# When the blocks of a seven-product pair are loaded: the fifth made unit's block one unit in front of the pair, and one group of sums one unit later

## The chip, the cores and the metric

The kernel runs on one core of a Trainium2 chip. The metric is the device time of one execution in microseconds. The kernel before has a median of 2097.52 us over three runs (2096.82 to 2102.56); its profiled execution took 2096.35 us, of which 2094.6 us are the profile's span.

## The reference

Two transformer layers over 256 tokens of 2048 channels, in float32. What matters here is the multilayer perceptron at the end of each layer, which reads two matrices of 2048x8192 and 8192x2048:

```python
def sq_relu_mlp(h, g, w1, w2):
    a = jax.nn.relu(rms_norm(h, g) @ w1)
    return (a * a) @ w2

h = h + o.reshape(B, S, D) @ a_w_out[l]
h = h + sq_relu_mlp(h, mlp_norm_g[layer], mlp_w1[layer], mlp_w2[layer])
```

In front of each perceptron stands an attention with its projections (a causal one with a forget gate in the first layer, a chunked one with a relative bias in the second), and between the layers one K/V projection. The change touches the two perceptrons alone.

## The kernel before

**Units.** All weights stream from memory. A weight tile of 128x1024 is a unit. ScalarE rounds it to `hi` (line 218), VectorE subtracts to get `lo` (line 219), and TensorE makes three passes, `hi` by the rounded activations (462), `hi` by their rest (464), `lo` by the rounded activations (466). Three `hi` and three `lo` buffers exist, so the splitting can run some units ahead of TensorE and no further. Plain units come into four `raw` buffers by SyncE's queue (line 201), `EARLY` = 3 of them in front of the splitting, which itself is kept `AHEAD` = 2 units in front of the products by `top_up`.

**Pairs.** In the perceptrons the weights are taken two column blocks at a time, a pair, and a pair's first rows are multiplied by a scheme with seven products in place of eight. For it four blocks of the pair, `"11"`, `"12"`, `"21"`, `"22"`, are loaded whole into rooms of their own by `bring` (line 801), and seven made units are formed from them, in the order

```python
self.pair, self.name, self.half = pair, ("11", "T3", "T2", "T1", "21", "T4", "22")[i], half
```

where `T3` = 22 + 12, `T2` = T3 + 11, `T1` = 12 + 11, `T4` = 21 + T2. Pairs are plain (blocks of 128x1024) or wide (128x1536, a second half unit `hih`, `loh` of 512 columns goes with each made unit). In a wide pair VectorE makes `T3` and `T2` (`make`, line 811) while `T1` and `T4` are made by a transfer that adds a block from memory onto a tile (`put`, line 817, GpSimd's queue). In a plain pair VectorE makes all four. All rooms have two buffers to a tag: `"12"` and `"21"` share one tag, `"11"` and `"22"` the other.

**Order around a pair.** `Pair.plan` writes out the order: made units 1 to 4, with the last three plain units of the pair before between them, then the pair's own plain units with made units 5, 6 and 7 among the first of them. The fifth made unit is block `"21"`. Each pair also has a tuple `when`, in the order `("12", "22", "21", "11", "T3", "T1")`, which says how many plain units ahead of the pair's start each block is loaded, or `T3` and `T1` made; `prepare` is called after every plain unit with the count `d` of plain units left and does what is due. Since all engines but GpSimd keep the written order (`keep_order`), a block's load takes a fixed place among the `raw` loads and the small transfers of SyncE's one queue, and it is issued when everything written ahead of it there has been issued; a `raw` load waits there for a buffer that line 219 has to give free.

There are 16 pairs to a perceptron, eight of the first matrix (numbered `i` = 0 to 7, all wide but the first) and eight of the second (the odd ones wide). 15 of the 16 have one of the two tuples that are changed.

**Hidden activations.** When the two accumulators of a column block of the first matrix are complete, `turn_hidden` (the change's second place) turns them through memory (lines 330, 340, 346) and then runs seven steps at given plain units: relu, rounded square, square, rest of the square (line 841), the four sums of activations for the seven-product scheme (lines 285 to 288), their rounding (292), their rest (295). The tuple `uses` holds the units; the first chunk's first two column blocks have tuples of their own, of which one is changed.

Of the kernel before, what the change touches and what calls it, by code (L numbers as in the profile page):

```python
# [33 lines left out]
WIDE1 = (1, 2, 3, 4, 5, 6, 7)  # L34
# [15 lines left out]
def trunk(ctx: ExitStack, tc: tile.TileContext, xT, xr, gs, hg, bf, wgate, w_in, w_oa, w1a, w1fa, w1sa, w2a, w2fa, w2sa,  # L50
# [94 lines left out]
    def plan_mlp(w1, w1f, w1s, w2, w2f, w2s, tail):  # L145
        pairs = []

        def add(w, wf, ws, i, wides, order, when):
            j = wides.index(i) if i in wides else i - sum(1 for k in wides if k < i)
            names = ("11", "12", "21", "22")  # L150
            if i in wides:
                src = [[None] * 3 + [ws[10 * j + 5 * q + u] for u in range(5)] for q in range(2)]
                big = {k: wf[4 * j + m] for m, k in enumerate(names)}
            else:
                src = [[w[16 * j + 8 * q + u] for u in range(8)] for q in range(2)]
                big = {k: src[int(k[1]) - 1][int(k[0]) - 1] for k in names}
            pairs.append(Pair(big, src, order, len(pairs) % 2 == 0, when, i in wides))

        close = (7, 5, 6, 4, 3, 2)
        for c in range(NCH):  # L160
            for q in range(2):
                i = 2 * c + q
                order = "ahead" if i in WIDE1 else "" if i else "early"
                when = (25, 20, 9, 15, 10, 8) if not i else (9, 7, 8, 6, 3, 2) if i == 1 else close if i - 1 in WIDE1 or not q else (9, 7, 8, 6, 5, 1)
                add(w1, w1f, w1s, i, WIDE1, order, when)
            for q in range(2):
                i = 2 * c + q
                add(w2, w2f, w2s, i, WIDE2, "wide" if q else "late", close if q or i + 1 in WIDE1 else (9, 7, 8, 6, 5, 2))
        plan, rest = [], [(tail, 0, u) for u in range(KT // UA - 3, KT // UA)]
        for p in pairs:  # L170
            mine, rest = p.plan(rest)
            plan += mine
        plan += rest
        units.extend(Form(p, i, q == 3) if q > 1 else p.src[q][i] for p, q, i in plan)
        return plan
# [4 lines left out]
    queue(w_oa, n_out)  # L180
    tail_a = Tail(w_oa, n_out - 5)
    plan_a = plan_mlp(w1a, w1fa, w1sa, w2a, w2fa, w2sa, tail_a)
    queue(w_qb, w_qb.shape[0])
    for i in range(w_kv.shape[0]):
        units.append(w_kv[i])
    queue(w_ob, n_out)
    tail_b = Tail(w_ob, n_out - 5)
    plan_b = plan_mlp(w1b, w1fb, w1sb, w2b, w2fb, w2sb, tail_b)
    ready = deque()

# [127 lines left out]
    def steps(make):  # L318
        box = []

        def step():
            if not box:
                box.append(make())
            next(box[0])
        return step

    def blocks32(src, z, b):
        n = src.shape[1] // P
        nb = z.shape[1] // (n * P)
        V.transpose(z.rearrange("p (j n b c) -> p b n j c", j=4, n=n, b=nb)[:, b],  # L330
                    src.rearrange("p (n j c) -> p n j c", n=n, j=4))

    def carry(z, dst, wait=1):
        w = z.shape[1]
        n = w // 4
        box = []

        def rows():
            box.append(dram.tile([P, w], F32, name="turn", tag=f"turn{w}", bufs=4))
            SY.dma_start(box[0], z)  # L340

        def columns():
            s = box[0].rearrange("(i a) f -> a i f", i=4)
            d = dst.rearrange("p (i f) -> p i f", i=4)
            for j in range(4):
                SY.dma_start(d[32 * j : 32 * j + 32], s[:, :, j * n : (j + 1) * n])

        return [[rows]] + [[]] * wait + [[columns], [], []]

    def turned(name=None):  # L350
        z = qkv.tile([P, GH * T], F32, name="z")
        return (z, qkv.tile([P, GH * T], F32, name=name, tag=name, bufs=2)) if name else z
# [310 lines left out]
    def add_fill(items):  # L663
        for i, it in enumerate(items):
            if i < len(fill):
                fill[i] = fill[i] + it
            else:
                fill.append(it)
# [155 lines left out]
    def mlp(plan, x, Sx, st, last):  # L824
# [4 lines left out]
        def take(t, c, n):  # L829
            S.activation(t, t, AF.Relu)  # L830
            y = acts.tile([P, 2, GH, T], F32R, name="act")
            hi, lo = (y[:, i].rearrange("p k (b i c) -> p (k b) i c", b=NB, i=4) for i in range(2))
            t3 = t.rearrange("p (i kb c) -> p kb i c", i=4, c=32)
            yield
            S.activation(hi, t3, AF.Square)
            yield
            S.activation(t, t, AF.Square)
            yield

            def low():  # L840
                V.tensor_tensor(lo, t3, hi.bitcast(F32), op=ALU.subtract)

            hids[c].extend(y[:, :, j, :] for j in range(GH))
            low()
            yield
            if n == 0:
                r = prob.tile([P, 9 * 3 * P], F32R, name="Sh", tag="p", bufs=1)
                Sh[c].extend(r[:, i : i + n] for i, n in ((0, UN), (UN, UN), (2 * UN, 512), (2 * UN + 512, 512)))
                yield from sums([[t3[:, 2 * j + b :: 4] for j in range(2)] for b in range(NB)], Sh[c])
            elif n == 1:  # L850
                yield from sums([[t3[:, 2 * j + b : 2 * j + b + 1] for j in range(2)] for b in range(NB)], Sh[c][2:], 1)

        def turn_hidden(c, n):
            zt = []

            def f(b, ps):
                if b == 0:
                    zt.extend(turned("q"))
                blocks32(ps, zt[0], b)
                if b == NB - 1:  # L860
                    step = steps(lambda: take(zt[1], c, n))
                    uses = ((4, 5, 7, 8, 9, 10, 11), (4, 5, 6, 7, 8, 10, 15), (4, 5, 7, 8), (4, 5, 6, 6))[n]
                    if not c and n < 2:
                        uses = (5, 6, 7, 8, 8, 10, 15) if n else (4, 5, 6, 7, 8, 9, 10)
                    add_fill(carry(*zt, 0)[:2] + [[step] * uses.count(i) for i in range(3, uses[-1] + 1)])
            return f

# [192 lines left out]
```

## Time and profile before

| | |
|---|---|
| median of 3 runs | 2097.52 us (2096.82 to 2102.56) |
| profiled execution | 2096.35 us, span 2094.6 us |
| TensorE matmuls (PE) | 2087.4 us busy, 100% of the span, 9266 of them |
| TensorE weight loads (PEld) | 1726.7 us, 82% |
| VectorE (DVE) | 1606.3 us, 77% |
| ScalarE (ACT) | 1233.0 us, 59% |
| GpSimd (POOL) | 98.2 us, 5% |
| HBM read and written | 250 GB/s over the span |
| granted TensorE clock | 1.00 |

Engine names in the profile are those in brackets; SPq is SyncE's queue of transfers, and L219 is line 219 of the kernel. A row of the timeline has the start and the length in us, the engine, the line, the operation, the tiles it writes and reads, how many equal instructions were merged (x4), and in brackets how long the engine had been idle and what ended that. The length of a matmul there is a modelled one that overlaps its successor; the distance between starts is the pace. A transfer's row shows its issue; it lands later.

### The profile page before, as it was taken

To read this page: it belongs to the slowest core of one execution; us is meant where nothing else is said; L and a number is where in the kernel's file an instruction comes from. 1 tells how busy PE (TensorE), PEld (TensorE's weight loads), DVE (VectorE), ACT (ScalarE), POOL (GpSimd) and SP (SyncE) were. 2 spreads that over 40 slices of the span, in tenths; PEclk is the share of its full clock that TensorE was granted. 3 is DMA by queue.
4 is the path that set the end of the run, shared out by engine and by line. 5 is a ranking of instruction groups with operands and counts; after the bars stand their busy time and mean duration, and the time that the engine had idled before them with its cause. 6 is when DMAs were issued, how large, how long until landed. Compare 5 with 4: busy or idle time off the path is not lost.

```text
span 2094.6 us, 26203 instructions
## 1 busy us (share of the span) xinstructions
PE 2087.4 (100%) x9266; PEld 1726.7 (82%) x9266; DVE 1606.3 (77%) x1920; ACT 1233.0 (59%) x1583; POOL 98.2 (5%) x107
## 2 busy tenths in 40 slices
PE   9999999999999999999999999999999999999999
PEld 7888888888888888888888888887888888888887
DVE  6767666888788778878777677678977887788786
ACT  6544454776566566556675455456755665665664
POOL 1111000000000000000001010000000000000000
PEclk9999999999999999999999999999999999999999
DMA  7787778778787897787778777788787887878875
GB/s 287 246 257 242 228 255 266 250 253 276 250 265 236 260 277 251 220 276 271 230 233 263 236 233 232 240 268 256 250 279 250 243 261 256 269 244 247 275 265 152
DMA packets 181205, 526.25 MB, mean 251 GB/s; under 512 B 36801, under 2 KB 72017, under 8 KB 181073
## 3 DMA queue, kind: packets, MB, share of 16 engines
q1 hardware_dynamic: 173552, 484.69, 68.3%
q0 software_dynamic: 7520, 39.87, 10.2%
q8 instruction: 73, 1.20, 0.2%
q14 instruction: 60, 0.48, 0.1%
HBM read 484.62 MB, written 39.87 MB: 250 GB/s over the span
## 4 chain that ended last, share of the span: by engine, by line
PE 98%; DMA 1%; ACT 0%; DVE 0%; SPq 0%; issue 0%; DVEq 0%; ACTq 0%
PE acc L462 26%; PE acc L464 26%; PE acc L466 26%; PE s L466 6%; PE s L462 6%; PE s L464 6%; PE s L605 1%; PE po L635 1%; DMA raw<-in_w1b 0%; PE s L604 0%; PE po L636 0%; DMA raw<-in_w_in 0%; PE s L727 0%; ACT hi L218 0%; DVE lo L219 0%; DVE act L310 0%
## 5 line engine op out<-in xcount | busy, mean ns | idle before, releaser
L219 DVE TENSOR_TENSOR lo<-raw,hi 128x1024 fp32r<-128x1024 f32 (+1 forms) x598 | 724.7, 1216 | 241.5 <-ACT hi L218 227.0
L218 ACT ACTIVATE hi<-raw 128x1024 fp32r<-128x1024 f32 (+1 forms) x598 | 628.6, 1052 | 318.1 <-PE acc L464 231.7
L462 PE MATMUL acc<-hi,act 128*128 128x512 f32 x2154 | 593.1, 394 | 2.0 <-ACT act L309 1.1
L464 PE MATMUL acc<-hi,act 128*128 128x512 f32 x2154 | 583.8, 389 | 0.1
L466 PE MATMUL acc<-lo,act 128*128 128x512 f32 x2154 | 583.2, 389 | 0.1
L464 PEld LDWEIGHTS acc<-hi,act 128*128 128x128 f32 x2154 | 403.9, 188 | 85.7 <-DVE act L310 0.7
L466 PEld LDWEIGHTS acc<-lo,act 128*128 128x128 f32 x2154 | 403.8, 188 | 85.2 <-DVE lo L219 1.4
L462 PEld LDWEIGHTS acc<-hi,act 128*128 128x128 f32 x2154 | 401.7, 188 | 85.6 <-ACT hi L218 1.7
L218 ACT ACTIVATE hi<-w 128x1024 fp32r<-128x1024 f32 x138 | 145.6, 1055 | 126.3 <-DMA w<-in_w1fb 26.8
L219 DVE TENSOR_TENSOR lo<-w,hi 128x1024 fp32r<-128x1024 f32 x138 | 167.6, 1214 | 54.5 <-ACT hi L218 48.6
L219 DVE TENSOR_TENSOR lo<-wT,hi 128x1024 fp32r<-128x1024 f32 x86 | 104.9, 1219 | 37.0 <-ACT hi L218 36.6
L462 PE MATMUL s<-hi,act 128*128 128x512 f32 x424 | 114.7, 389 | 0.0
L466 PE MATMUL s<-lo,act 128*128 128x512 f32 x424 | 114.6, 389 | 0.0
L464 PE MATMUL s<-hi,act 128*128 128x512 f32 x424 | 114.6, 389 | 0.0
L218 ACT ACTIVATE hi<-wT 128x1024 fp32r<-128x1024 f32 x86 | 90.8, 1056 | 24.8 <-PE acc L464 13.0
L464 PEld LDWEIGHTS s<-hi,act 128*128 128x128 f32 x424 | 79.6, 188 | 16.5
L466 PEld LDWEIGHTS s<-lo,act 128*128 128x128 f32 x424 | 79.4, 188 | 16.7 <-DVE lo L219 0.2
L462 PEld LDWEIGHTS s<-hi,act 128*128 128x128 f32 x424 | 79.5, 188 | 16.5
L218 ACT ACTIVATE hih<-w 128x512 fp32r<-128x512 f32 x88 | 55.2, 627 | 61.0 <-PE acc L464 50.0
L219 DVE TENSOR_TENSOR loh<-w,hih 128x512 fp32r<-128x512 f32 x88 | 60.4, 687 | 19.8 <-ACT hih L218 19.8
L218 ACT ACTIVATE hih<-wT 128x512 fp32r<-128x512 f32 x66 | 41.4, 628 | 57.2 <-PE acc L464 47.9
L638 ACT ACTIVATE act<-po 128x256 fp32r<-128x256 f32 x32 | 12.3, 385 | 86.2 <-PE po L636 86.2
(207 smaller groups left out, 1835.4 us busy)
## 6 DMA issues: line engine op xcount, KB each, us to landing
raw<-in_w_in SPq DMA_DIRECT2D x96, 512.0 KB, 4.5
raw<-in_w1sa SPq DMA_DIRECT2D x70, 512.0 KB, 5.5
raw<-in_w1sb SPq DMA_DIRECT2D x70, 512.0 KB, 5.8
raw<-in_w_kv SPq DMA_DIRECT2D x64, 512.0 KB, 4.6
turn<-z SPq DMA_DIRECT2D x60, 512.0 KB, 4.2
raw<-in_w2a SPq DMA_DIRECT2D x48, 512.0 KB, 5.2
raw<-in_w2b SPq DMA_DIRECT2D x48, 512.0 KB, 5.3
q<-turn SPq DMA_DIRECT2D x168, 128.0 KB, 3.8
```

Of the source, the lines that this page charges most:

```text
L218: S.activation(hi[:, c], raw[:, c], AF.Copy)
L219: V.tensor_tensor(lo[:, c], raw[:, c], hi[:, c].bitcast(F32), op=ALU.subtract)
L462: TE.matmul(ps[:, cols], xh, cut(hi, j), start=first, stop=False, **kw)
L464: TE.matmul(ps[:, cols], xl, cut(hi, j), start=False, stop=False, **kw)
L466: TE.matmul(ps[:, cols], xh, cut(lo, j), start=False, stop=last, **kw)
L605: TE.matmul(s[:, P : 3 * P], q[:, a, P:T], k[:, a], start=True, stop=True)
L635: TE.matmul(po[:, :T], v[:, 0, a * P : (a + 1) * P], pT[:, :2], start=True, stop=False)
L638: S.activation(o[i][:, 0], po[:, :T], AF.Copy)
```

## The change

In the tuple `close` and in that of the first matrix's second pair, block `"21"` is loaded 1 plain unit in front of the pair instead of 6 or 8. In the second of these, block `"11"` is also loaded at 5 instead of 6. In the first chunk's second column block, the four sums run at plain unit 9 instead of 8; the steps before and after them stay.

```diff
-        close = (7, 5, 6, 4, 3, 2)
+        close = (7, 5, 1, 4, 3, 2)
         for c in range(NCH):
             for q in range(2):
                 i = 2 * c + q
                 order = "ahead" if i in WIDE1 else "" if i else "early"
-                when = (25, 20, 9, 15, 10, 8) if not i else (9, 7, 8, 6, 3, 2) if i == 1 else close if i - 1 in WIDE1 or not q else (9, 7, 8, 6, 5, 1)
+                when = (25, 20, 9, 15, 10, 8) if not i else (9, 7, 1, 5, 3, 2) if i == 1 else close if i - 1 in WIDE1 or not q else (9, 7, 8, 6, 5, 1)
...
                     if not c and n < 2:
-                        uses = (5, 6, 7, 8, 8, 10, 15) if n else (4, 5, 6, 7, 8, 9, 10)
+                        uses = (5, 6, 7, 8, 9, 10, 15) if n else (4, 5, 6, 7, 8, 9, 10)
```

No instruction is added or removed on TensorE, VectorE, ScalarE or in the number and size of transfers: 30 loads of a block (15 pairs in each of two layers) move in SyncE's order, two loads of `"11"` move by one `raw` load, and two groups of four sums move in VectorE's order.

## The prediction

> **What bounds the kernel now.** I read the page first, then busy time by stretches, then TensorE's waits, and only then the queues.
>
> ```profile
> span 2094.6 us, 26203 instructions
> PE 2087.4 (100%) x9266; PEld 1726.7 (82%) x9266; DVE 1606.3 (77%) x1920; ACT 1233.0 (59%) x1583; POOL 98.2 (5%) x107
> ...
> q1 hardware_dynamic: 173552, 484.69, 68.3%
> ```
>
> ```profile
> core 0: us, PE busy (x) PEld busy (x) DVE busy (x) ACT busy (x) POOL busy (x), PEclk, DMA share, GB/s
> ...
> 380.00:1010.00 630.00, 630.00 (x2778) 520.72 (x2777) 513.03 (x536) 394.86 (x465) 17.91 (x21) 1.00 0.80 257
> 1010.00:1420.00 410.00, 409.86 (x1841) 340.26 (x1841) 292.30 (x419) 228.07 (x337) 27.94 (x26) 1.00 0.78 244
> 1420.00:2060.00 640.00, 638.76 (x2811) 526.30 (x2810) 520.61 (x546) 397.69 (x466) 18.68 (x22) 1.00 0.81 256
> ```
>
> ```profile
> PE acc L462 <- ACT act L309: 1.1, 1, 1.1
> ...
> PE acc L462 <- ACT hi L218: 0.8, 1, 0.8
> ```
>
> The changed loads lie in the two perceptrons, about 380 to 1010 us and 1420 to 2060 us. TensorE is busy for 630.00 of 630.00 us in the first and for 638.76 of 640.00 in the second: 1.24 us idle. Its list of waits has these two on weights and activations; the 1.1 us are the second perceptron's, the 0.8 us fall in the kernel's first microseconds, out of reach of the change. A busy matmul's end is modelled, so the pace has to be looked at too; the timeline of TensorE at that wait shows it:
>
> ```profile
> 1446.82 1.07 PE L464 MATMUL acc<-hi,act 128*128 128x512 f32 x4
> 1447.73 1.07 PE L466 MATMUL acc<-lo,act 128*128 128x512 f32 x4
> 1449.88 1.20 PE L462 MATMUL acc<-hi,act 128*128 128x512 f32 x4 [1.08 <-ACT act L309]
> 1451.14 1.19 PE L464 MATMUL acc<-hi,act 128*128 128x512 f32 x4
> 1452.16 1.09 PE L466 MATMUL acc<-lo,act 128*128 128x512 f32 x4
> ```
>
> Four matmuls start every 0.905 us when nothing is missing (1446.82 to 1447.73), 226 ns each. The granted clock is 1.00 in all three stretches, and the change takes no matmul away. So the perceptrons can give back only what stands above this pace, a few microseconds, while every load that arrives late enough can add to the time. 0.3% of 2097.5 us, about what a measurement of this kernel can tell from no change, is 6.3 us.
>
> The Trainium skill (Perfetto Trace Analysis, Identifying the Most-Contended Engine) says that matmul busy time is no good measure of the distance to the roofline, and that the share of weight loads should be taken instead. By that share, an estimate, 2094.6 - 1726.7 = 368 us would be open. The even pace between the starts decides against it here: no load that comes earlier makes a matmul start sooner.
>
> **What the removed load frees in front of the first made unit.** The one real stall lies at 1448 us, at the start of the second layer's second pair. ScalarE, then SyncE's queue:
>
> ```profile
> 1441.89 1.06 ACT L218 ACTIVATE hi<-raw 128x1024 fp32r<-128x1024 f32 x1 [3.33 <-DMA raw<-in_w1b]
> ...
> 1446.88 1.06 ACT L218 ACTIVATE hi<-raw 128x1024 fp32r<-128x1024 f32 x1 [2.28 <-DMA raw<-in_w1b]
> ...
> 1448.77 1.06 ACT L309 ACTIVATE act<-y 128x1024 fp32r<-128x1024 f32 x1
> ```
>
> ```profile
> 1431.50 0.42 SPq L801 DMA_DIRECT2D w<-in_w1fb  x1
> ...
> 1436.87 0.48 SPq L801 DMA_DIRECT2D w<-in_w1fb  x1
> ...
> 1441.80 0.33 SPq L801 DMA_DIRECT2D w<-in_w1fb  x1
> ```
>
> ScalarE stood 3.33 and 2.28 us for plain units that came late, because three whole blocks of 768 KB were issued among them in ten microseconds. The first of these three, at 1431.50, is block "21"; the change takes it out to behind 1452 us. What a block costs its neighbours: hardware queue q1 moved 484.69 MB in 68.3% of the span, so 0.339 MB a microsecond, and 0.786 MB take 2.3 us of all engines. The two waits of 5.6 us together should shrink by about that, and TensorE's start at 1449.88 comes back to its pace. Its loss: 1449.88 - 1447.73 - 0.905 = 1.24 us, then 1451.14 - 1449.88 - 0.905 = 0.36, then 0.12; together 1.7 us.
>
> The same edit acts at every wide pair of the second matrix, where blocks "21", "22" and "11" follow each other within 4.1 us. One of the eight, and the costliest:
>
> ```profile
> 1523.87 0.43 SPq L801 DMA_DIRECT2D w<-in_w2fb  x1
> ...
> 1525.68 1.05 SPq L801 DMA_DIRECT2D w<-in_w2fb  x1
> ...
> 1527.95 0.47 SPq L801 DMA_DIRECT2D w<-in_w2fb  x1
> ```
>
> ```profile
> 1538.61 1.06 ACT L218 ACTIVATE hi<-w 128x1024 fp32r<-128x1024 f32 x1 [6.88 <-DMA w<-in_w2fb]
> ```
>
> ```profile
> 1538.63 1.07 PE L466 MATMUL acc<-lo,act 128*128 128x512 f32 x4
> 1539.73 0.73 PE L462 MATMUL acc<-hi,act 128*128 128x512 f32 x2
> 1540.30 0.62 PE L464 MATMUL acc<-hi,act 128*128 128x512 f32 x2
> 1540.99 0.73 PE L466 MATMUL acc<-lo,act 128*128 128x512 f32 x2
> ```
>
> ScalarE waits 6.88 us for block "11", and its lead over TensorE is just used up: 1539.73 is 0.20 late, 1540.30 is 0.12 late (two matmuls take 0.453), 1540.99 is 0.24 late, 0.55 us in all. Without "21" in the queue, "11" lands up to 2.3 us earlier, the wait is nearer 4.6 us, and the 0.55 us go. In the other pairs such waits cost ScalarE idle time and TensorE nothing, so their shortening is worth nothing. Both places give at most 1.7 + 0.55 = 2.3 us; nothing gained is the other bound. I take 2.0, near the upper end, since both losses sit behind the very queue that is relieved.
>
> **What the moved load meets.** In the changed order block "21" goes out directly ahead of the raw load that is issued at 750.97 us in the tightest wide pair, and of the one at 1498.29 in a plain pair; in the latter the four `q<-turn` transfers, which wait for their rows to land, stand ahead of it. Who needs it, how long blocks take to land (min/median/max, all of line 801), and what else is in flight:
>
> ```profile
> 750.97 10.41 SPq L201 DMA_DIRECT2D raw<-in_w1sa  x3
> ```
>
> ```profile
> 1498.29 13.41 SPq L201 DMA_DIRECT2D raw<-in_w2b  x4
> ```
>
> ```profile
> 764.85 1.04 ACT L218 ACTIVATE hi<-w 128x1024 fp32r<-128x1024 f32 x1
> ```
>
> ```profile
> 1507.26 1.22 DVE L811 TENSOR_TENSOR w<-w,wT 128x1024 f32<-128x1024 f32 x1
> ```
>
> ```profile
> DMA to landing us min/median/max: 3.4/6.7/10.6
> ```
>
> Wide: 764.85 - 750.97 = 13.9 us for a landing of 6.7, at worst 10.6; no wait. Plain: 1507.26 - 1498.29 = 9.0 us until VectorE adds it into T4; 2.3 us over the median, and 1.6 under the worst. A worst landing would hold VectorE, and queued behind this addition are a sum in PSUM and the next `lo`, which TensorE needs. I take zero by the median, and a cost of up to 1.6 us a plain pair, eight of them, 12.8 us, as the far end, which the range does not follow to its end since it needs the worst landing every time. The raw loads behind the moved block start some 0.4 us later in the queue and land up to 2.3 us later; they are three units ahead of their use, 8 us at 12 matmuls of 226 ns a unit, so nothing waits.
>
> The four sums of the first chunk's second block:
>
> ```profile
> 1504.79 0.28 DVE L288 TENSOR_TENSOR sum<-q,sum 128x128 f32<-128x128 f32 x1
> ...
> 1504.99 1.22 DVE L219 TENSOR_TENSOR lo<-wT,hi 128x1024 fp32r<-128x1024 f32 x1
> 1506.12 1.22 DVE L219 TENSOR_TENSOR lo<-raw,hi 128x1024 fp32r<-128x1024 f32 x1
> ```
>
> They pass behind these two `lo`, about 2.3 us later, and in front of the addition at 1507.26, whose time stays. Their rounding on ScalarE stays a unit behind. The two `lo` come about 0.9 us sooner, which can only help; two such places, taken as zero.
>
> Sum: the profiled execution's 2096.35 less 2.0 is 2094.4 us. The median of the runs lies 1.2 above the profiled one; the prediction for the median is 2097.5 - 2.0 = 2095.5 us.
>
> **Rivals.** *Slower: the fifth block collides with T1.* T1 is made by GpSimd's transfer, issued two units in front of the pair, and the block now goes out one unit in front, into it:
>
> ```profile
> 747.03 0.84 POOL L817 DMA_DIRECT2D w<-in_w1fa  x1 [27.71 <-ACT hih L218]
> ```
>
> ```profile
> 760.97 1.04 ACT L218 ACTIVATE hi<-w 128x1024 fp32r<-128x1024 f32 x1
> ```
>
> ```profile
> DMA to landing us min/median/max: 6.8/7.4/10.5
> ```
>
> This one lands at the latest figure, 747.03 + 10.5 = 757.5, and is read at 760.97: 3.4 us to spare. The block adds 2.3 us of traffic, so 1.1 are left; the rival decides from the point where a put loses more than 3.4 us. If sharing costs it twice the block's time, 4.6 us, then 1.2 us are missing; in each of six such pairs (the fourth, sixth and eighth of the first matrix, both layers), were all as tight as this one and TensorE without any lead to absorb it, that is 7.2: 2097.5 + 7.2 = 2104.7. The spread from 6.8 to 10.5 under today's traffic speaks for it, the 3.4 us to spare against. The next transfer of this kind, T4's, has little to spare, but it goes out late:
>
> ```profile
> 759.94 0.86 POOL L817 DMA_DIRECT2D wT<-in_w1fa  x1 [12.07 <-DVE loh L219]
> ```
>
> By then the block, at 750.97 + 6.7 = 757.7, has landed; only the worst landing, 761.6, would overlap it, by 1.7 us.
>
> The Trainium skill (DMA: Bandwidth & Descriptors, Queues, rings and completion order) says that each DMA engine takes turns between queues, packet by packet. By that rule the put and the block alternate and the put loses at most the block's own 2.3 us, which is inside the spare time. The trace shows that puts do stretch, 10.5 against 6.8 us, and cannot show this pairing.
>
> *The waits don't move.* Block "11" lands as late as before since raw loads, not "21", keep the queue full: 2097.5.
>
> *Faster than the pace allows*, as the weight-load share would have it: if arrivals, not the array, set the 226 ns, earlier blocks could save over 6.3 us, below 2091.2. Nothing in the rows supports it.
>
> **How the numbers follow.** Forecast 0.81, waits that don't move 0.09; both lie within 0.3%: 0.90. Collision, or its like in the plain pairs, 0.08: slower. Faster 0.02. The range starts at the profiled time less all 2.3 us, 2094.0, and goes up past the unmoved 2097.5 to 2100.5, 0.1 us of stall in each of 30 moved loads.
>
> **What would show it.** Right: TensorE's waits without the 1.1 us of L309; busy 640.00 of 640.00 in the second stretch; the wait of 6.88 us before block "11" at under 5; puts of line 817 landing by 11 us; no wait of VectorE's line 811 on a block. Wrong: a row in which TensorE waits for L218 or L219 at a third or fourth made unit, behind a put that lands 14 us or more after its issue, or total idle in the two stretches above 6 us.

## The result, and the profile after

| | before | changed |
|---|---|---|
| median of 20 runs | 2098.61 us (2095.74 to 2104.81) | 2094.61 us (2093.66 to 2095.82) |
| profiled execution | 2096.35 us, span 2094.6 | 2093.66 us, span 2091.9 |

The ratio of changed to before is 0.9979, 95% interval 0.9972 to 0.9986: 4.0 us faster in the median, within 0.3%, inside the range of 2094.0 to 2100.5 and 0.9 us under the 2095.5 forecast. The gain is twice the 2.0 us that was forecast: over 20 runs the kernel before has a median 1.1 us above that of the three runs from which the forecast was counted. Note the spread: the runs before cover 9 us, the changed ones 2.2.

Busy time by stretches and TensorE's whole list of waits, changed kernel:

```profile
core 0: us, PE busy (x) PEld busy (x) DVE busy (x) ACT busy (x) POOL busy (x), PEclk, DMA share, GB/s
...
380.00:1010.00 630.00, 629.67 (x2778) 520.62 (x2777) 512.95 (x536) 395.28 (x466) 17.93 (x21) 1.00 0.80 257
...
1420.00:2060.00 640.00, 639.67 (x2821) 528.88 (x2820) 522.98 (x549) 399.94 (x469) 18.68 (x22) 1.00 0.81 257
```

```profile
PE acc L462 <- ACT hi L218: 1.3, 1, 1.3
PE pt L91 <- DVE mhalf L93: 1.1, 1, 1.1
PE s L462 <- DVE acc L893: 0.7, 2, 0.3
```

The second perceptron's idle time fell from 1.24 to 0.33 us, and the wait on line 309 is gone. But the first perceptron, which had none, now has 0.33 too. Both are the last row, which is new: TensorE waits twice for the sum in PSUM of line 893. (The first two rows lie in the kernel's first microseconds, as before.)

The place of the old stall, changed kernel, ScalarE, TensorE and SyncE's queue:

```profile
1444.30 1.06 ACT L218 ACTIVATE hi<-raw 128x1024 fp32r<-128x1024 f32 x1 [2.96 <-DMA raw<-in_w1b]
...
1448.70 1.06 ACT L218 ACTIVATE hi<-w 128x1024 fp32r<-128x1024 f32 x1 [0.50 <-DMA w<-in_w1fb]
```

```profile
1446.53 1.07 PE L464 MATMUL acc<-hi,act 128*128 128x512 f32 x4
1447.44 1.07 PE L466 MATMUL acc<-lo,act 128*128 128x512 f32 x4
1448.35 1.07 PE L462 MATMUL acc<-hi,act 128*128 128x512 f32 x4
```

```profile
1435.93 0.43 SPq L801 DMA_DIRECT2D w<-in_w1fb  x1
...
1440.01 0.51 SPq L801 DMA_DIRECT2D w<-in_w1fb  x1
...
1450.05 0.42 SPq L801 DMA_DIRECT2D w<-in_w1fb  x1
```

Blocks "22" and "11" are left in the stretch, "21" goes out at 1450.05. ScalarE's waits of 3.33 and 2.28 us there became one of 2.96 and one of 0.50, 2.2 us less together where 2.3 were forecast, and TensorE starts at its pace of 0.905 us.

The wide pair of 1538 us before, now at 1535 us, waits less for block "11":

```profile
1535.44 1.06 ACT L218 ACTIVATE hi<-w 128x1024 fp32r<-128x1024 f32 x1 [5.05 <-DMA w<-in_w2fb]
```

### The profile page after: what moved, and what is told of

It reads as the page before. It is cut to its first block, busy times and chain, and to the rows that moved or that the text cites. A ratio compares the mean times of both kernels' runs of the same rounds, so it can differ in the third digit from the quotient of the medians.

```text
span 2091.9 us, 26247 instructions
## 1 busy us (share of the span) xinstructions
PE 2084.8 (100%) x9266; PEld 1727.2 (83%) x9266; DVE 1606.5 (77%) x1920; ACT 1234.2 (59%) x1583; POOL 97.5 (5%) x107
## 2 busy tenths in 40 slices
DMA packets 181204, 526.25 MB, mean 252 GB/s; under 512 B 36800, under 2 KB 72016, under 8 KB 181072
## 4 chain that ended last, share of the span: by engine, by line
PE 99%; DVE 1%; DMA 0%; ACT 0%; issue 0%; SPq 0%; DVEq 0%; ACTq 0%
PE acc L462 26%; PE acc L464 26%; PE acc L466 26%; PE s L462 6%; PE s L466 6%; PE s L464 6%; PE s L605 1%; PE po L635 1%; PE s L604 0%; PE po L636 0%; DVE lo L219 0%; DMA raw<-in_w_in 0%; PE s L727 0%; ACT hi L218 0%; DVE w L811 0%
```

## Experiments: which load it is

Two kernels split the loads: the second pair's tuple alone, and the tuple `close` alone.

```diff
# e3, second pair alone
-(9, 7, 8, 6, 3, 2) if i == 1
+(9, 7, 1, 5, 3, 2) if i == 1
# e4, close alone
-close = (7, 5, 6, 4, 3, 2)
+close = (7, 5, 1, 4, 3, 2)
```

> The kernel before with only the second pair's tuple changed, (9, 7, 1, 5, 3, 2), in each of the two layers. Theory (the one large stall sits at the second layer's second pair): the stall of 1.7 us near 1449 us is gone, the 0.55 us near 1540 us stay, and the median falls by 1.7 us or more, since executions with later transfers lose more there. Rival (the gain is spread over the other 28 pairs): the median falls by under 0.8 us.

> The kernel before with only the tuple close changed (28 pairs). Theory (the large stall is the second pair's): TensorE's wait near 1449 us stays at 1 us or more, the 0.55 us near 1540 us and 0.2 to 0.3 us at 834, 1672 and 2005 us go, and the median falls by 0.6 to 1.4 us. Rival (the 28 pairs carry the gain): the median falls by 3 us or more.

Measured, on the same chip: the second pair alone 2094.62 us (2093.07 to 2097.49), ratio to before 0.9981, interval 0.9971 to 0.9990; `close` alone 2098.05 us (2095.55 to 2102.13), ratio 1.0000, interval 0.9991 to 1.0008. Two loads of 30 carry the gain that these runs resolve; what the other 28 are worth lies within 2 us either way by this interval. TensorE with `close` alone, at the second layer's second pair, shows what an execution loses there:

```profile
1449.53 1.07 PE L466 MATMUL acc<-lo,act 128*128 128x512 f32 x4
1452.12 1.19 PE L462 MATMUL acc<-hi,act 128*128 128x512 f32 x4 [1.52 <-ACT act L309]
1453.38 1.92 PE L464 MATMUL acc<-hi,act 128*128 128x512 f32 x4
1455.10 1.91 PE L466 MATMUL acc<-lo,act 128*128 128x512 f32 x4
1456.80 1.18 PE L462 MATMUL acc<-hi,act 128*128 128x512 f32 x4
1457.82 1.08 PE L464 MATMUL acc<-hi,act 128*128 128x512 f32 x4
```

1452.12 - 1449.53 - 0.905 = 1.69 us, then 0.36, 0.82, 0.80 and 0.12: 3.8 us in all, against 1.7 in the profile before. In this execution the first layer's second pair stalls as well, which the profile of before did not do; its list of waits for TensorE:

```profile
PE acc L462 <- ACT act L309: 3.0, 2, 1.5
```

The expectation for `close`, 0.6 to 1.4 us, is neither met nor refuted: its median is 0.87 us under the 2098.92 of the kernel before beside it, and the ratio is 1.0000. The 0.55 us near 1540 us were one execution's: the second pair alone, which leaves those loads where they were, loses next to nothing there, against its expectation. The traces lean towards a small gain. All of them hold the same 9266 matmuls in the same order, so their starts can be compared one by one. In the two perceptrons, outside the second pairs and the two places of the moved sums, the profiled execution of the fastest kernel below (the changed one without the moved sums) is the standard: six kernels with `close` unmoved lose 1.0 to 3.1 us against it, five more executions with it moved, that of `close` alone among them, 0.0 to 1.3. These are single executions, so about 1 us for `close` is likely and not shown.

Then the two changes inside the second pair's tuple, and the distance:

```diff
# e5: block 21 alone
+(9, 7, 1, 6, 3, 2) if i == 1
# e6: block 11 alone
+(9, 7, 8, 5, 3, 2) if i == 1
# e7: block 21 alone, at 4
+(9, 7, 4, 6, 3, 2) if i == 1
```

> The kernel before with block 21 of the second pair alone at 1 (block 11 stays at 6), both layers. Theory (the block's 2.3 us of traffic among the plain units make the stall): no wait of TensorE at the second pairs, median within 0.6 us of the 2094.6 of the whole second-pair tuple. Rival (block 11's step behind one more plain unit does it): stalls of 1 to 4 us at 408 or 1449 us stay, median within 1 us of the kernel before.

> The kernel before with block 11 of the second pair alone at 5 (block 21 stays at 8), both layers. Theory (21 is the cause): the stalls at 408 or 1449 us stay, median within 1 us of the kernel before. Rival (11 is the cause): they go, median 3 to 4 us below.

> The kernel before with block 21 of the second pair alone at 4, which is behind block 11 and two plain units. Theory (it has only to leave the stretch with the turned rows and the three blocks; how late it comes doesn't matter): as with 1, median 3 to 4 us below the kernel before. Rival (it has to come one unit in front of the pair, since the two plain units behind 11 need the bandwidth too): half of the gain or less, and a wait of ScalarE on a plain unit of 2 us or more remains in front of the pair.

Measured beside each other: "21" at 1, 2094.45 us (ratio 0.9983, interval 0.9973 to 0.9993); "11" at 5, 2098.81 us (0.9998, 0.9988 to 1.0008), with the stall in its profile; "21" at 4, 2094.68 us (0.9984, 0.9974 to 0.9994). Where "21" alone moved, TensorE's list has no wait on line 309. So it is block "21", and it has only to be behind "11" and two plain units; one unit in front of the pair is not needed.

```profile
1449.56 1.07 PE L466 MATMUL acc<-lo,act 128*128 128x512 f32 x4
1452.60 1.19 PE L462 MATMUL acc<-hi,act 128*128 128x512 f32 x4 [1.97 <-ACT act L309]
```

These are TensorE's rows with "11" alone moved: 2.13 us over the pace in one start.

## Experiments: what the moved sums cost

The changed kernel with the sums back at unit 8, and the kernel before with the sums alone moved:

```diff
# e1 and e10: the changed kernel, but
-uses = (5, 6, 7, 8, 9, 10, 15)
+uses = (5, 6, 7, 8, 8, 10, 15)
# e2: the kernel before, but
-uses = (5, 6, 7, 8, 8, 10, 15)
+uses = (5, 6, 7, 8, 9, 10, 15)
```

> The changed kernel with the four sums back at unit 8. Theory (the loads are the gain, the moved sums are a cost of 0.49 us at each of the two places where TensorE now waits for the sum of line 893): both waits of 0.3 us on line 893 are gone from TensorE's list, and the median is 1.0 us under the changed kernel's 2094.61, at 2093.6. Rival (the waits on line 893 come from block 21 landing later, not from the sums): both waits stay and the median stays at 2094.6.

> The kernel before with only the four sums at unit 9. Theory (moved sums cost): TensorE waits for line 893 near 469 and 1509 us, 0.2 to 0.5 us each, and the median is 0.4 to 1.0 us above the kernel before beside it. Rival (the sums are neutral, as the prediction had it, or help, since two lo come 0.9 us sooner): no such wait, median within 0.3 us of the kernel before, or below it.

Loads only: 2094.3 us (2092.8 to 2097.18), ratio 0.9976, interval 0.9967 to 0.9985, no wait on line 893. Sums only: 2099.17 us against 2098.92, ratio 0.9997, interval 0.9989 to 1.0006, with both waits:

```profile
PE s L462 <- DVE acc L893: 0.7, 2, 0.4
```

The wait follows the sums and not the loads. Its cost in time is not settled by these medians: beside the 4.5 us spread of runs with the old stall a microsecond is lost. So the changed kernel and loads only ran beside each other:

> The changed kernel itself, beside the next run, to settle what the moved sums cost. Theory (each of the two places costs 0.49 us): two waits on line 893, and the median stands 0.5 to 1.0 us above the next run's. Rival (the waits are real but small beside the spread of the runs, or the next run pays elsewhere): medians within 0.3 us.

> The changed kernel with the four sums at unit 8. Theory: no wait on line 893, 0.5 to 1.0 us under the changed kernel beside it. Rival: within 0.3 us of it.

On another chip: changed 2095.01 us (2093.80 to 2096.08), ratio to before 0.9985, interval 0.9976 to 0.9993; loads only 2093.39 us (2092.97 to 2094.23), 0.9973, interval 0.9964 to 0.9982. The moved sums cost 1.6 us, more than the 0.5 to 1.0 that was expected; the two ranges hardly overlap. The two waits that the profile shows come to 2 x 0.49 us over the pace (1507.99 - 1506.60 - 0.905 below), and the 14 matmuls between 1507.99 and 1511.44 lose 0.28 us more (3.45 - 14 x 0.905 / 4): 0.77 us at a place, 1.5 at both. Loads only loses a little there too: 0.28 us over the 14 between 1503.41 and 1506.86, from the pass at 1504.43 on, which starts just after the end of the `lo` of 1503.16. Counted start by start the two profiles differ by 1.0 us at the two places; where the remaining 0.6 of the medians lie was not located.

How, VectorE's rows in the changed kernel and in loads only (its second measurement), then TensorE in the same order:

```profile
1501.14 1.22 DVE L841 TENSOR_TENSOR act<-q,act 128x1024 fp32r<-128x1024 f32 x1
1502.49 1.22 DVE L219 TENSOR_TENSOR lo<-wT,hi 128x1024 fp32r<-128x1024 f32 x1
1503.95 1.22 DVE L219 TENSOR_TENSOR lo<-raw,hi 128x1024 fp32r<-128x1024 f32 x1 [0.23 <-ACT hi L218]
1505.09 0.28 DVE L285 TENSOR_TENSOR sum<-q 128x128 f32<-128x128 f32 x1
...
1507.16 0.69 DVE L893 SCALAR_TENSOR_TENSOR acc<-s,p 128x512 f32<-128x512 f32 x1
```

```profile
1502.22 0.28 DVE L285 TENSOR_TENSOR sum<-q 128x128 f32<-128x128 f32 x1
...
1503.16 1.22 DVE L219 TENSOR_TENSOR lo<-wT,hi 128x1024 fp32r<-128x1024 f32 x1
1504.29 1.22 DVE L219 TENSOR_TENSOR lo<-raw,hi 128x1024 fp32r<-128x1024 f32 x1
...
1506.56 0.69 DVE L893 SCALAR_TENSOR_TENSOR acc<-s,p 128x512 f32<-128x512 f32 x1
```

```profile
1506.60 1.07 PE L466 MATMUL acc<-lo,act 128*128 128x512 f32 x4
1507.99 0.70 PE L462 MATMUL s<-hi,Sh 128*128 128x512 f32 x2 [0.33 <-DVE acc L893]
...
1511.44 1.07 PE L466 MATMUL acc<-lo,act 128*128 128x512 f32 x4
```

```profile
1503.41 0.62 PE L462 MATMUL s<-hi,Sh 128*128 128x512 f32 x2
...
1504.43 0.74 PE L466 MATMUL s<-lo,Sh 128*128 128x512 f32 x2
...
1506.86 1.07 PE L466 MATMUL acc<-lo,act 128*128 128x512 f32 x4
1507.77 0.62 PE L462 MATMUL s<-hi,Sh 128*128 128x512 f32 x2
```

With the sums at 8 they fill the time in which VectorE would wait for ScalarE's next `hi`. Moved behind the two `lo`, that time stands empty (0.23 us before 1503.95, and some between 1501.14 and 1502.49), the two `lo` come only 0.67 and 0.34 us sooner, the sums are done later, and the sum of line 893 behind them starts 0.6 us later by the span's clock. It now ends at 1507.85, after TensorE wanted to start at 1507.51.

## Experiments: how much room the moved loads have

Each moved load of "21" issued twice in a row (sums at 8):

```diff
         SY.dma_start(p.t[name][:, : WIDE if p.wide else UN], p.big[name])
+        if name == "21" and p.units[2] == 1:
+            SY.dma_start(p.t[name][:, : WIDE if p.wide else UN], p.big[name])
```

> The loads of the change, sums at unit 8, and each moved load of block 21 issued twice in a row, which adds 30 loads of 0.5 or 0.79 MB, 1.5 to 2.3 us of all DMA engines each, right beside T1's transfer. Theory (the collision has room): TensorE's waits stay under 2 us in all, median within 1.5 us of 2094.3, the latest transfer of line 817 lands 11 to 13 us after its issue. Rival (the collision bites from 3.4 us on): six or more waits of TensorE on L218 or L219 behind T1, median 5 us or more above 2094.3.

Measured: 2102.01 us (2099.76 to 2109.27), ratio to before 1.0022, interval 1.0011 to 1.0034; 7.7 us above the 2094.3 of the same kernel without the second load, which ran in an earlier group on the same chip. The theory's "within 1.5 us" was wrong. First the transfers of T1 (out `w`) and T4 (out `wT`) with their sizes and median landings, before, then changed:

```profile
w<-in_w1fa POOLq DMA_DIRECT2D x7, 768.0 KB, 8.4
w<-in_w2fa POOLq DMA_DIRECT2D x4, 768.0 KB, 6.9
wT<-in_w2fa POOLq DMA_DIRECT2D x4, 768.0 KB, 7.2
```

```profile
w<-in_w1fa POOLq DMA_DIRECT2D x7, 768.0 KB, 9.2
w<-in_w2fa POOLq DMA_DIRECT2D x4, 768.0 KB, 9.6
```

At the wide pairs of the second matrix the moved block does slow T1's transfer, and T1 has the room: six profiles with `close` moved have medians of 8.9 to 9.7 us there, six with it unmoved 6.8 to 7.8, 2.2 us apart in the mean. At those of the first matrix the medians overlap (7.6 to 9.8 and 7.9 to 9.4), so the 0.8 us above alone show nothing. No engine is listed as waiting for a T1, before or after. With the block twice, its landings (min/median/max, both kinds) and the wait they cause:

```profile
DMA to landing us min/median/max: 7.0/8.7/12.2
```

```profile
ACT hi L218 <- DMA wT<-in_w1fa: 12.2, 3, 5.1
```

The late ones are `wT`, T4's, and not T1's: the six that took longest are all `wT`, and ScalarE waits for five of them, 20.3 us in all and up to 5.1 at once, for no T1. T4's transfer has little room: its readers waited for two even in the kernel before, 0.9 us each. That traffic piles up until it goes out is the likely reason and not shown. TensorE's listed waits are still small here, 1.6 us on `hi` and 1.0 on `lo`. Start by start it falls 7.6 us behind the kernel that loads the block once, in nine places: 1.3 us right behind a late `wT` (at 774 and 942 us), 1.1 behind a plain unit for which ScalarE waited 3.8 us (at 1814), 1.0 at the two places of the sums. The other 4.2 us, in four places, can't be put down to one transfer, so the late T4 explains only a part.

Last, block "21" of the tuple `close` at 3, behind "11" and in front of T1's transfer (sums at 8):

```diff
-close = (7, 5, 1, 4, 3, 2)
+close = (7, 5, 3, 4, 3, 2)
```

> The loads of the change with sums at unit 8, and in the tuple close block 21 at 3, behind block 11 and in front of T1's transfer, instead of 1. Theory (the 28 pairs of close gain nothing in time, and T1's transfers, which the change stretched from 8 to 9.5 us, have room): T1 lands in 7 to 9 us, block 11 still waits less than before, median within 0.5 us of the kernel beside it with 1. Rival (the stretch of T1's transfer costs hidden time): 1 us or more faster than with 1.

2093.66 us (2092.52 to 2095.28), ratio 0.9978, interval 0.9969 to 0.9987, beside 2093.39 with 1: no difference. All transfers of line 817 took 7.1 to 10.2 us with a median of 7.9, against 6.9 to 10.7 and 7.6 in the run beside it, so the position in front of T1 doesn't shorten them, against the expectation. T1 stayed stretched (9.0 to 9.4 us in the median), so this run can't price the stretch; that it costs nothing is read from the missing waits alone.

The version that beats both kernels is the changed one without the moved sums: 2093.39 us, 0.9973 of before.

## Why the prediction was right, and where its terms were off

*The bound.* Right: TensorE's pace holds, the busy time of both perceptrons is within 0.33 us of whole, and no run of any kernel here lies under 2092.5 us. The Trainium skill's share of weight loads (Perfetto Trace Analysis, Identifying the Most-Contended Engine) stands at 83% in the changed kernel; by that share 17% would still be open, and these runs show none of it.

*The second pair's stall, 1.7 us.* The mechanism was right, "21" among the plain units, and shown by moving it alone. The term was mis-sized: it was read from one execution, in which the first layer's second pair happened not to stall and the second lost little. In the median it is worth 3.4 to 4.3 us (e7, e5 and e3 against the before beside each), about twice the 2.0 of the whole sum. The sign was there to read: the three runs shown already went up to 2102.56, 6 us over the profiled one. Much of such a spread is this stall: other runs of the kernel before go down to 2093.17, the changed kernel's level. Not all of it is: the slowest run of loads only, 2097.18, was profiled, has no stall, and had fallen 3.1 us behind the 2093.11 execution of the same kernel within its first 30 us.

*The wide pairs of the second matrix, 0.55 us.* The shortening came, 6.88 to 5.05 us where 4.6 was estimated and under 5 was named as a sign, but the 0.55 are not shown to be a term of the median: `close` alone gives nothing that these runs resolve.

*The moved block's need.* Right: VectorE's line 811 shows 0.4 us of waiting on blocks in all after the change, not quite the none that was named as a sign, and 11.2 before; no wait of TensorE stands behind "21".

*The sums, zero, "which can only help".* Wrong, by 1.6 us. The step that failed is the count of what is queued: I looked at the addition at 1507.26, held that its time stays, and took the two `lo` that come sooner for a gain. They come 0.67 and 0.34 us sooner and not 0.9, since their `hi` aren't there; the sums had been filling that wait, and the addition moved back by 0.6 us with the sum of line 893 behind it. The prediction had named that sum as queued there, but only in the price of a late block. The two waits on it are also why the second stretch is busy for 639.67 us and not for the 640.00 that was named as a sign. The two errors have opposite signs, and the three runs' median was 1.1 us low: that the forecast came within 0.9 us of the result is in part luck.

*The collision.* The collision exists and costs nothing: T1 is stretched, clearly at the wide pairs of the second matrix, less clearly in the first matrix, where the six priced pairs lie, and no engine waits for it; with the block twice ScalarE waits for T4's transfers and for no T1, and even that accounts for a part of the loss only. The Trainium skill's turn-taking between queues (DMA: Bandwidth & Descriptors, Queues, rings and completion order) would have T1 lose at most the block's 2.3 us; measured 2.2 in the mean of twelve profiles where the stretch is clear, so these runs agree with it, other loads being moved in time as well.

## What to carry to other kernels

When the bounding engine is gapless, count what stands above its pace and stop looking for more; but size a stall that hangs on landing times by the spread of the runs, not by the one execution that was profiled. Look at where a large prefetch stands in the one queue that also carries the stream: behind the last load that is needed sooner was enough here. And before moving small work "out of the way", see whether it is filling a wait: moved, it leaves the hole and lands on something else's path.

## What was not expected

A 768 KB block that is issued in the same stretch as two others can cost its neighbours more than its own 2.3 us: with it left in place, TensorE lost 3.8 us at one pair of one execution. In the median the two blocks moved, one a layer, are worth 3.4 to 4.3 us, less than twice 2.3. That a plain unit's lateness also holds the small turned rows and the next plain units behind it in the same queue is the likely reason, and not shown. And the runs' spread itself fell: from 9 us to 2.2, with the same traffic of 526.25 MB; on the other chip from 8.8 and 9.5 us to 3.8 to 4.9 with "21" of the second pair moved.
